# Where the end of each feature group's conditioning and the next group's first weight splits stand in the order of a decoder-layer kernel

## The chip, the cores and the metric

One program on one core of a Trainium2 chip. The metric is device time in microseconds (us) per execution. The kernel before was timed three times: 1342.04 us median, 1340.69 lowest, 1342.91 highest.

## The reference, cut to what matters

One decoder layer is computed for 288 tokens together: 256 of a prompt and 8 sequences of 4 tokens. What matters here is its head:

```
mod = silu(c) @ w_ada + b_ada                  # 2048 -> 6 * 2048, one row per request (9 rows)
sh1, sc1, g1, sh2, sc2, g2 = split(mod, 6)
h = rmsnorm(x, norm1) * (1 + sc1) + sh1        # 288 x 2048
proj = h @ w_in                                # columns: pool | z | x,B,C | dt
```

After it come a pooling mixer, a causal convolution with a state-space scan, an output projection, a gated residual, a second modulated norm and a gated feed-forward part. Everything is float32; the results are the 288 x 2048 output and the new states.

## The kernel before, in words

**Layout.** Features lie on the 128 partitions and tokens on the free axis, so x is 16 tiles (k = 0 to 15) of 128 x 288. All weights come from one flat array, `wflat`, in the order in which they are used, in loads of 128 x 1024 float32 (`load`, L232, 512 KB each, issued by SP into 14 rotating buffers, `raw`).

**Three products for one.** A weight chunk is split into two rounded parts: the high part is a cast on ACT (`split`, L241), the low part is the difference on DVE (L242; on GpSimd for the chunks in `PSPLIT`). There are three buffers for split chunks (`wsp`) in this stage. The activations are split alike into `h1k` (high by ACT L448, low by DVE L449). `mm3` then runs three matmuls on TensorE (PE) for each tile and k: high x high (L263), high x low (L264), low x high (L265).

**Feature groups.** The projection cannot start on a feature tile before that tile's scale and shift are known, and those need a 2048-long product with `w_ada`. So the 16 feature tiles are cut into six groups (`KGROUPS`): tiles 0; 1; 2-3; 4-7; 8-11; 12-15. While PE multiplies group g's features with the weights of 28 output tiles (`xbc_units`, tiles m = 0 to 27), it also computes the conditioning of group g+1 (`ada_group_units`): `VISIT` names after which tiles a *visit* is made. A visit is a run of matmuls `adag` (L343) over several `w_ada` loads.

**The end of a conditioning** is what follows the last visit: the sums go from PSUM to SBUF on ACT (`asb_g`, L298), are transposed on PE (`adat_g`, L304, or a small product, L357), and become the multiplier and the shift on DVE (`amul` L370, `ada` L373). Then `modulate1` makes the operand of the next group: on ACT `h` of the prompt tokens (L446) and the high part (L448), on DVE two operations for the short sequences (L442, L443) and the low part (L449). The program text does both once tile 28 - `MOD[g]` has been written, so MOD is how many tiles ahead of the group's end the operand is written.

**Evictions.** A finished output tile is added from PSUM to its place in SBUF by DVE (L655), two operations for most tiles (256 prompt columns, 32 others), one for a `zy` tile (for group 0 these are copies, most of them on ACT). Output tiles use two PSUM pools: 3 buffers (`mm`) for m % 7 <= 2 and 4 buffers (`aux`) for the others; the transposes of the conditioning take one of the four.

**What sets the order.** A scheduler turns the program into one list of instructions for each engine; each engine takes its list in that order. Program order gives the priority; `tc.high_priority()` raises that of what is issued inside it, as `split` and `modulate1` do. `kpo` keeps an instruction in program order. `tc.issue_after(i)` puts what is issued inside the block behind instruction i, if it is of i's engine. The change rests on these.

Of the kernel before, what the change touches and what calls it, by code (L numbers as in the profile page):

```python
# [11 lines left out]
F32 = mybir.dt.float32  # L12
F32R = mybir.dt.float32r
AF = mybir.ActivationFunctionType
ALU = mybir.AluOpType
PSUM = bass.MemoryType.PSUM

P = 128
# [6 lines left out]
NC9 = 1 + NB  # L25
# [12 lines left out]
WU = (14, 2, 6)  # L38
# [2 lines left out]
SPLIT1, SPLIT2 = 2, 2  # L41
PHASE = (128, 32, 0, 128)
YK = 2
VISIT = {1: (4, (10,)), 2: (4, (7, 15)), 3: (4, (4, 9, 14, 19)), 4: (8, (8, 19)), 5: (8, (8, 19))}
PSPLIT = {1: (1, 2, 3), 2: (0,)}
MOD = (10, 8, 6, 6, 6)
AY = 2

RA1, RA2, RB1, RB2, RB3 = 0.5, 0.4, 1.0, 1.0, 1.0
# [89 lines left out]
def kernel(ctx: ExitStack, tc, ins, outs):  # L139
    nc = tc.nc  # L140
# [8 lines left out]
    def aux(name):  # L149
        return px.tile([P, 512], F32, tag="aux", name=name)  # L150
# [31 lines left out]
    def warm_pe(n, rhs=None):  # L182

        for _ in range(n):
            nc.tensor.matmul(wps[:, :P], ones, ones if rhs is None else rhs, start=True, stop=True)

    xhi = [None]
    xlo = [None]
# [59 lines left out]
    def split_hi():  # L248
        pair = wp[0].tile([P, WSC], F32R, tag="wsp", name="wsp_xbc0_0")
        hi, lo = pair[:, WH:WH + RAWC], pair[:, WL:WL + RAWC]  # L250
        raw = load(("xbc", 0, 0))
        kpo(nc.scalar.copy(hi, raw))
        return hi, lo, raw

    def split_xbc(gi, ci, pin=False):
        (ks, ms), key = _xbc_chunks(gi)[ci], ("xbc", gi, ci)
        return ready.pop(key, None) or split(load(key), 0, len(ms) * len(ks) * P, f"xbc{gi}_{ci}",
                                             nc.gpsimd if ci in PSPLIT.get(gi, ()) else None, pin)
# [37 lines left out]
    def ada_sb(ps, nb, name, r=P, pin=lambda i: i):  # L296
        asb = kp.tile([P, 512], F32, tag="asb", name="asb_" + name)
        pin(nc.scalar.copy(asb[0:r, :nb], ps[0:r, :nb]))  # L298
        return asb

    def ada_tr(asb, nb, name, r=P):
        pt = aux("adat_" + name)
        for i in range(nb // P):
            nc.tensor.transpose(pt[:, i * r:(i + 1) * r], asb[0:r, i * P:(i + 1) * P], ident[0:r, 0:r])  # L304
        return pt
# [7 lines left out]
    def ada_group_units(gi):  # L313

        k0, gk = KGROUPS[gi]
        nj = min(2 * gk, 4)
        nb = 2 * gk * P // nj
        per = RAWC // (nj * nb)
        ps = pa.tile([P, 512], F32, tag="ada", name=f"adag{gi}")
        nq = KT // per  # L320

        def steps(q, raw):
            if gk == 1:
                for kk in range(0, per, 2):
                    for j in range(4):
                        yield j, q * per + kk + j // 2, raw[:, kk * 256 + j * P:kk * 256 + j * P + P]
            else:
                for kk in range(per):
                    for j in range(nj):
                        c = (kk * nj + j) * nb  # L330
                        yield j, q * per + kk, raw[:, c:c + nb]

        n = 0
        visit = VISIT[gi][0] if gi else 1
        for v in range(0, nq, visit):
            raws = [(q, load(("ada", gi, q))) for q in range(v, v + visit)]
            if not gi:
                yield
            begun = False
            for q, raw in raws[::-1]:  # L340
                for j, k, w in steps(q, raw):
                    with tc.high_priority() if begun else nullcontext():
                        i = nc.tensor.matmul(ps[32 * j:32 * j + 32, :nb], sc_c[:, k, :], w, start=n < 4,  # L343
                                             stop=n >= (KT if gk > 1 else KT // 2) * 4 - 4,
                                             tile_position=(0, 32 * j))
                    if begun:
                        tc.keep_in_program_order(i)
                    begun = gi > 0
                    n += 1
            if gi:  # L350
                yield
        r = 32 * nj
        pin = kpo if gi == 0 else (lambda i: i)
        if gk == 1:
            asb = ada_sb(ps, nb, f"g{gi}", pin=pin)
            pt = aux(f"adat_g{gi}")
            nc.tensor.matmul(pt[:, :r], asb[:, :nb], early[:, K_S2:K_S2 + r], start=True, stop=True)  # L357
            if gi == 0:
                warm_pe(WU[2], asb[:, 0:P])
                first.append(split_hi())  # L360
        else:
            pt = ada_tr(ada_sb(ps, nb, f"g{gi}", r), nb, f"g{gi}", r)
        for i in range(nb // P):

            o = ada[:, 0:2, k0:k0 + gk, :].rearrange("p a (b i) c -> p a b i c", b=nj // 2)[:, :, :, i, :]
            b = bada[:, 0:2, k0:k0 + gk].rearrange("p a (b i) -> p a b i", b=nj // 2)[:, :, :, i]
            src = pt[:, i * r:(i + 1) * r].rearrange("p (a b c) -> p a b c", a=2, b=nj // 2)[:, :, :, 0:NC9]
            for j in range(nj // 2):
                k = k0 + j * (nb // P) + i
                pin(nc.vector.tensor_scalar(amul[:, 0, k, :], src[:, 1, j, :], early[:, V_N1 + k:V_N1 + k + 1],  # L370
                                            nb1[:, k:k + 1], ALU.mult, ALU.add))
            o, src, b = o[:, 0], src[:, 0], b[:, 0]
            pin(nc.vector.tensor_tensor(o, src, b.unsqueeze(2).to_broadcast([P, nj // 2, NC9]), ALU.add))  # L373

    def ada_part_units(part, ay=1):
        ps = pa.tile([P, 512], F32, tag="ada", name=f"adap{part}")
# [48 lines left out]
    def normalize(k0, gk, r):  # L425
        xv = xav(k0, gk)
        kpo(nc.vector.tensor_tensor(xv, xv, r.unsqueeze(1).to_broadcast([P, gk, N]), ALU.mult))

    def modulate1(k0, gk, name):

        h = kp.tile([P, 4, N], F32, tag="hmod", name="h_" + name, bufs=2)
        xv = xav(k0, gk)
        pin = kpo if k0 == 0 else (lambda i: i)
        with tc.high_priority():
            hs = h[:, :gk, NP:N].rearrange("p k (b l) -> p k b l", b=NB)
            xs = xv[:, :, NP:N].rearrange("p k (b l) -> p k b l", b=NB)
            sa = amul[:, 0, k0:k0 + gk, 1:NC9].unsqueeze(3).to_broadcast([P, gk, NB, NL])
            sb = ada[:, 0, k0:k0 + gk, 1:NC9].unsqueeze(3).to_broadcast([P, gk, NB, NL])
            if k0 == 0:
                kpo(nc.vector.tensor_scalar(h[:, 0, 0:NP], xv[:, 0, 0:NP], amul[:, 0, 0, 0:1], ada[:, 0, 0, 0:1],  # L440
                                            ALU.mult, ALU.add))
            pin(nc.vector.tensor_tensor(hs, xs, sa, ALU.mult))  # L442
            pin(nc.vector.tensor_tensor(hs, hs, sb, ALU.add))  # L443
            for i in range(gk):
                if k0:
                    nc.scalar.activation(h[:, i, 0:NP], xv[:, i, 0:NP], AF.Identity,  # L446
                                         scale=amul[:, 0, k0 + i, 0:1], bias=ada[:, 0, k0 + i, 0:1])
                pin(nc.scalar.copy(xhi[0][k0 + i], h[:, i, :]))  # L448
                pin(nc.vector.tensor_tensor(xlo[0][k0 + i], h[:, i, :], xhi[0][k0 + i].bitcast(F32), ALU.subtract))  # L449


    class _W:
# [178 lines left out]
    def xbc_units(gi):  # L631
        k0, gk = KGROUPS[gi]
        for ci, (ks, ms) in enumerate(_xbc_chunks(gi)):
            hi, lo = split_xbc(gi, ci)
            for b, m in enumerate(ms):
                wide = gi < len(KGROUPS) - 1 and m % 7 > 2
                ps = aux(f"xbc{gi}_{m}") if wide else pm.tile([P, 512], F32, tag="mm", name=f"xbc{gi}_{m}")
                for i, k in enumerate(ks):
                    mm3(ps[:, :N], hi, lo, b * gk + i, xhi[0][k], xlo[0][k], i == 0, i == gk - 1)
                if m < XT:  # L640
                    g, r = divmod(m, 5)
                    parts = [(cvp[g][:, r, 3:3 + NP], ps[:, 0:NP]), (cvs(g)[:, r, :, 3:7], samp(ps[:, NP:N]))]
                elif m < XT + len(UEARLY):
                    u = UEARLY[m - XT]
                    parts = [(upp[:, u, 15:], ps[:, 0:NP]), (ups[:, u, :, 15:19], samp(ps[:, NP:N]))]
                else:
                    g, t = divmod(m - XT - len(UEARLY), 3)
                    parts = [(zy[g][:, t, :], ps[:, 0:N])]
                for o, v in parts:
                    if gi == 0 and m % 7 == 5:  # L650
                        nc.vector.tensor_copy(o, v)
                    elif gi == 0:
                        nc.scalar.copy(o, v)
                    else:
                        nc.vector.tensor_tensor(o, o, v, ALU.add)  # L655
                yield m
# [727 lines left out]
```

## Time and profile before

| what | value |
|---|---|
| median of three runs | 1342.04 us |
| the profiled execution's own time | 1342.67 us |
| its span in the profile | 1340.4 us |
| mean granted TensorE clock | 0.994 |
| ACT busy | 580.3 us (43%) |
| DVE busy | 818.6 us (61%) |
| GpSimd (POOL) busy | 232.0 us (17%) |
| moved by DMA | 323.25 MB, mean 241 GB/s |

PE and PEld are TensorE's matmuls and weight loads, SP the engine that issues the loads. In a table of stages, a stretch is given as from:to in us from the span's start, then its length, the busy time of each engine with its count of instructions, the granted TensorE clock (1.00 is full speed, 0.50 half), the mean busy share of the DMA engines and GB/s. In a list of instructions in order of time a row is start, length, engine, line, operation, out<-in, shapes and, in brackets, the idle time just before it and what ended it; neighbours of the same kind are merged (x2). A row of waits is engine, what waited, what it waited for, and us in total, times, longest. Names are shown without buffer numbers, so `xbc` at L263 may be a tile of one group or of the next.

Groups 0 to 5 begin on TensorE at about 19.9, 34.9, 53.0, 87.2, 141 and 192 us.

### The profile page before, as it was taken

What the parts mean: (1) busy time and instruction counts of PE and PEld (TensorE: products, weight loads), DVE (VectorE), ACT (ScalarE), POOL (GpSimd) and SP (SyncE); (2) the same over time, 40 slices, a digit from 0 to 9 for tenths busy, and PEclk for the clock granted to TensorE, in tenths of its full rate; (3) what the DMA queues carried; (4) which work ended last, traced back from release to release, by engine and by line L of the source; (5) the groups of instructions that cost most, each with busy time, mean ns of one, the idle gap of its engine ahead of it and who ended that gap; (6) DMA issues with size and microseconds to landing.
All of it is one profiled execution on the core that took longest, in us unless ns stands there. A gap on an engine that the chain in (4) does not pass through costs nothing.

```text
span 1340.4 us, 26255 instructions
## 1 busy us (share of the span) xinstructions
PE 1316.9 (98%) x10541; PEld 1230.7 (92%) x10541; DVE 818.6 (61%) x1458; ACT 580.3 (43%) x934; POOL 232.0 (17%) x420
## 2 busy tenths in 40 slices
PE   8999999999999999999999999999999999999997
PEld 7888997777778889999999999999999999999997
DVE  5675658888674448745665545666664566566553
ACT  5332434579643334533443333434433344344452
POOL 0201001223222123101221001312220011132221
PEclk9999999999999999999999999999999999999999
DMA  9997888888888967787655556656555666666641
GB/s 375 365 370 303 337 272 306 313 318 322 313 315 326 328 241 262 243 297 279 196 184 186 168 172 192 204 188 195 179 184 169 185 197 185 201 195 200 188 122 71
DMA packets 97193, 323.25 MB, mean 241 GB/s; under 512 B 10736, under 2 KB 19760, under 8 KB 97072
## 3 DMA queue, kind: packets, MB, share of 16 engines
q1 hardware_dynamic: 93168, 310.70, 67.4%
q0 software_dynamic: 3184, 9.69, 2.0%
q8 instruction: 82, 1.34, 0.4%
q10 hardware_dynamic: 720, 1.19, 0.2%
q14 instruction: 39, 0.32, 0.1%
HBM read 309.84 MB, written 10.39 MB: 239 GB/s over the span
## 4 chain that ended last, share of the span: by engine, by line
PE 94%; DVE 2%; DMA 1%; ACT 1%; issue 1%; POOL 0%; SPq 0%; DVEq 0%; POOLq 0%; ACTq 0%
PE mm_down L263 7%; PE mm_down L265 7%; PE mm_down L264 7%; PE mm_gate L263 6%; PE mm_val L263 6%; PE mm_gate L264 6%; PE mm_val L264 6%; PE mm_gate L265 6%; PE mm_val L265 6%; PE xbc L263 4%; PE xbc L264 4%; PE xbc L265 4%; PE adap L384 4%; PE mm_out L263 3%; PE mm_out L264 2%; PE mm_out L265 2%
## 5 line engine op out<-in xcount | busy, mean ns | idle before, releaser
L264 PE MATMUL mm_down<-ahl,wsp_down 128*128 128x288 f32 x688 | 201.2, 292 | 0.0
L263 PE MATMUL mm_down<-ahl,wsp_down 128*128 128x288 f32 x688 | 201.0, 292 | 0.0
L265 PE MATMUL mm_down<-ahl,wsp_down 128*128 128x288 f32 x688 | 201.0, 292 | 0.0
L263 PE MATMUL mm_gate<-h2k,wsp_gate 128*128 128x288 f32 x640 | 187.6, 293 | 0.0
L264 PE MATMUL mm_gate<-h2k,wsp_gate 128*128 128x288 f32 x640 | 187.1, 292 | 0.0
L264 PE MATMUL mm_val<-h2k,wsp_val 128*128 128x288 f32 x640 | 187.0, 292 | 0.0
L263 PE MATMUL mm_val<-h2k,wsp_val 128*128 128x288 f32 x640 | 186.9, 292 | 0.0
L265 PE MATMUL mm_gate<-h2k,wsp_gate 128*128 128x288 f32 x640 | 186.1, 291 | 0.0
L265 PE MATMUL mm_val<-h2k,wsp_val 128*128 128x288 f32 x640 | 186.0, 291 | 0.0
L242 DVE TENSOR_TENSOR wsp_down<-raw_down,wsp_down 128x1024 fp32r<-128x1024 f32 x96 | 107.3, 1117 | 119.9 <-ACT wsp_down L241 119.0
L242 DVE TENSOR_TENSOR wsp_gate<-raw_gate,wsp_gate 128x1024 fp32r<-128x1024 f32 x80 | 98.3, 1230 | 128.8 <-ACT wsp_gate L241 128.8
L241 ACT CAST wsp_down<-raw_down 128x1024 fp32r<-128x1024 f32 x96 | 92.3, 961 | 165.3 <-PE mm_down L265 114.7
L241 ACT CAST wsp_gate<-raw_gate 128x1024 fp32r<-128x1024 f32 x80 | 83.8, 1049 | 152.5 <-PE mm_gate L265 69.3
L263 PE MATMUL xbc<-h1k,wsp_xbc 128*128 128x288 f32 x448 | 133.2, 302 | 5.1 <-ACT h1k L448 3.2
L241 ACT CAST wsp_val<-raw_val 128x1024 fp32r<-128x1024 f32 x80 | 84.0, 1050 | 122.5 <-issue 107.2
L264 PE MATMUL xbc<-h1k,wsp_xbc 128*128 128x288 f32 x448 | 132.1, 297 | 0.5 <-DVE h1k L449 0.5
L263 PEld LDWEIGHTS mm_down<-ahl,wsp_down 128*128 128x128 f32 x688 | 130.1, 189 | 0.0
L265 PEld LDWEIGHTS mm_down<-ahl,wsp_down 128*128 128x128 f32 x688 | 129.2, 188 | 0.0
L264 PEld LDWEIGHTS mm_down<-ahl,wsp_down 128*128 128x128 f32 x688 | 128.8, 187 | 0.0
L265 PE MATMUL xbc<-h1k,wsp_xbc 128*128 128x288 f32 x448 | 128.5, 294 | 0.0
L263 PEld LDWEIGHTS mm_gate<-h2k,wsp_gate 128*128 128x128 f32 x640 | 120.5, 188 | 5.0 <-ACT ahl L1149 4.2
L263 PEld LDWEIGHTS mm_val<-h2k,wsp_val 128*128 128x128 f32 x640 | 120.5, 188 | 0.0
(320 smaller groups left out, 2985.0 us busy)
## 6 DMA issues: line engine op xcount, KB each, us to landing
raw_adap<-wflat SPq DMA_DIRECT2D x128, 512.0 KB, 6.1
raw_gate<-wflat SPq DMA_DIRECT2D x80, 512.0 KB, 3.5
raw_val<-wflat SPq DMA_DIRECT2D x80, 512.0 KB, 3.6
raw_ada<-wflat SPq DMA_DIRECT2D x64, 512.0 KB, 9.2
raw_xbc<-wflat SPq DMA_DIRECT2D x55, 512.0 KB, 9.1
raw_down<-wflat SPq DMA_DIRECT2D x48, 512.0 KB, 3.6
raw_out<-wflat SPq DMA_DIRECT2D x32, 512.0 KB, 6.4
raw_down<-wflat SPq DMA_DIRECT2D x32, 384.0 KB, 3.1
```

The costliest lines, as they stand in the source:

```text
L241: i = nc.scalar.copy(hi[:, :n], raw[:, a:a + n])
L242: j = (eng or nc.vector).tensor_tensor(lo[:, :n], raw[:, a:a + n], hi[:, :n].bitcast(F32), ALU.subtract)
L263: nc.tensor.matmul(ps, whi[:, w], bh, start=first, stop=False)
L264: nc.tensor.matmul(ps, whi[:, w], bl, start=False, stop=False)
L265: nc.tensor.matmul(ps, wlo[:, w], bh, start=False, stop=last)
L384: i = nc.tensor.matmul(ps[32 * j:32 * j + 32, :512], sc_c[:, k, :], raw[:, (j % 2) * 512:(j % 2) * 512 + 512], start=(k == ay - 1), stop=( ...
```

## The change

Three edits. First, the end of each conditioning (`asb_g`, `adat_g`, `amul`, `ada`) is issued at high priority. Second, in groups 1 to 5 the splits of the second and third weight chunks are put behind the last high part (on ACT) and the last low part (on DVE) of that group's operand. Third, for the conditioning of group 3, which runs in group 2, the visits stand after tiles 4, 8, 12 and 16 in place of 4, 9, 14 and 19, and the operand is written nine tiles ahead of the group's end in place of six. Nothing is added or taken away: the same instructions run in another order. The body that the first edit indents is shown by its first lines.

```diff
-VISIT = {1: (4, (10,)), 2: (4, (7, 15)), 3: (4, (4, 9, 14, 19)), 4: (8, (8, 19)), 5: (8, (8, 19))}
+VISIT = {1: (4, (10,)), 2: (4, (7, 15)), 3: (4, (4, 8, 12, 16)), 4: (8, (8, 19)), 5: (8, (8, 19))}
-MOD = (10, 8, 6, 6, 6)
+MOD = (10, 8, 9, 6, 6)
...
-        r = 32 * nj
-        pin = kpo if gi == 0 else (lambda i: i)
-        if gk == 1:
-            asb = ada_sb(ps, nb, f"g{gi}", pin=pin)
+        with tc.high_priority():
+            r = 32 * nj
+            pin = kpo if gi == 0 else (lambda i: i)
+            if gk == 1:
+                asb = ada_sb(ps, nb, f"g{gi}", pin=pin)
...
+    behind = [None, None]
...
-                pin(nc.scalar.copy(xhi[0][k0 + i], h[:, i, :]))
-                pin(nc.vector.tensor_tensor(xlo[0][k0 + i], h[:, i, :], xhi[0][k0 + i].bitcast(F32), ALU.subtract))
+                behind[0] = pin(nc.scalar.copy(xhi[0][k0 + i], h[:, i, :]))
+                behind[1] = pin(nc.vector.tensor_tensor(xlo[0][k0 + i], h[:, i, :], xhi[0][k0 + i].bitcast(F32),
+                                                        ALU.subtract))
...
-            hi, lo = split_xbc(gi, ci)
+            if gi and ci in (1, 2):
+                with tc.issue_after(behind[0].ins), tc.issue_after(behind[1].ins):
+                    hi, lo = split_xbc(gi, ci)
+            else:
+                hi, lo = split_xbc(gi, ci)
```

Three places show what this does to the order. In all of them `wsp_xbc_1` is a split of weight chunk 1 of a group, `h1k_177` and the like are operands by feature tile (177 and 178 are those of group 2, 179 to 182 those of group 3), `asb_g`, `adat_g`, `amul`, `ada` and `h_g` are the steps of the conditioning and the operand, and `cvp`, `upp`, `ups` and `zy` are where evictions go.

DVE at the end of group 1, before:

```order
L655 TENSOR_TENSOR ups<-ups,xbc_20_717 128x8x4
L370 TENSOR_SCALAR amul<-adat_g_725,early,nb_82 128x9 x2
L242 TENSOR_TENSOR wsp_xbc_1_823<-raw_xbc_1_821,wsp_xbc_1_823 128x1024
L442 TENSOR_TENSOR h_g_730<-xa_92,amul 128x2x32
L373 TENSOR_TENSOR ada<-adat_g_725,early 128x18
L655 TENSOR_TENSOR upp<-upp,xbc_21_739 128x256
L443 TENSOR_TENSOR h_g_730<-h_g_730,ada 128x2x32
L655 TENSOR_TENSOR ups<-ups,xbc_21_739 128x8x4
L655 TENSOR_TENSOR zy_195<-zy_195,xbc_22_745 128x288
L655 TENSOR_TENSOR zy_195<-zy_195,xbc_23_750 128x288
L449 TENSOR_TENSOR h1k_177<-h_g_730,h1k_177 128x288
L449 TENSOR_TENSOR h1k_178<-h_g_730,h1k_178 128x288
```

The same place in the change:

```order
L663 TENSOR_TENSOR cvp_167<-cvp_167,xbc_18_705 128x256
L371 TENSOR_SCALAR amul<-adat_g_725,early,nb_82 128x9 x2
L374 TENSOR_TENSOR ada<-adat_g_725,early 128x18
L445 TENSOR_TENSOR h_g_730<-xa_92,amul 128x2x32
L663 TENSOR_TENSOR cvp_167<-cvp_167,xbc_18_705 128x8x4
L446 TENSOR_TENSOR h_g_730<-h_g_730,ada 128x2x32
L663 TENSOR_TENSOR cvp_167<-cvp_167,xbc_19_711 128x256
```

The end of the conditioning now stands behind the first half of tile 18's eviction, not behind tile 20's, and the split of chunk 1 no longer stands between `amul` and `ada`. Further down, both low parts of `h1k` come between the two halves of tile 21's eviction, and the split of chunk 1 comes after tile 22's.

ACT at the end of group 2, before:

```order
L298 COPY asb_g_1113<-adag_835 128x256
L241 CAST wsp_xbc_6_1149<-raw_xbc_6_1147 128x1024
L241 CAST wsp_xbc_0_1187<-raw_xbc_0_1185 128x1024
L446 ACTIVATE h_g_1124<-xa_94,ada,amul 128x256 x2
L241 CAST wsp_xbc_1_1222<-raw_xbc_1_1220 128x1024
L446 ACTIVATE h_g_1124<-xa_94,ada,amul 128x256 x2
L241 CAST wsp_xbc_2_1257<-raw_xbc_2_1255 128x1024
L448 CAST h1k_179<-h_g_1124 128x288
```

And in the change:

```order
L298 COPY asb_g_1082<-adag_835 128x256
L241 CAST wsp_xbc_6_1149<-raw_xbc_6_1147 128x1024
L449 ACTIVATE h_g_1093<-xa_94,ada,amul 128x256 x2
L241 CAST wsp_xbc_0_1187<-raw_xbc_0_1185 128x1024
L451 CAST h1k_179<-h_g_1093 128x288
L449 ACTIVATE h_g_1093<-xa_94,ada,amul 128x256 x2
L451 CAST h1k_180<-h_g_1093 128x288
L451 CAST h1k_181<-h_g_1093 128x288
L451 CAST h1k_182<-h_g_1093 128x288
L241 CAST wsp_xbc_1_1222<-raw_xbc_1_1220 128x1024
```

The casts of chunks 1 and 2 of group 3 went from ahead of the operand's four high parts to behind them.

DVE at the same place, before, from the first `ada` of the conditioning on:

```order
L373 TENSOR_TENSOR ada<-adat_g_1115,early 128x2x9
L370 TENSOR_SCALAR amul<-adat_g_1115,early,nb_82 128x9
L242 TENSOR_TENSOR wsp_xbc_0_1187<-raw_xbc_0_1185,wsp_xbc_0_1187 128x1024
L370 TENSOR_SCALAR amul<-adat_g_1115,early,nb_82 128x9
L373 TENSOR_TENSOR ada<-adat_g_1115,early 128x2x9
L442 TENSOR_TENSOR h_g_1124<-xa_94,amul 128x4x32
L655 TENSOR_TENSOR zy_195<-zy_195,xbc_23_1139 128x288
L443 TENSOR_TENSOR h_g_1124<-h_g_1124,ada 128x4x32
L242 TENSOR_TENSOR wsp_xbc_1_1222<-raw_xbc_1_1220,wsp_xbc_1_1222 128x1024
L655 TENSOR_TENSOR zy_195<-zy_195,xbc_24_1152 128x288
L242 TENSOR_TENSOR wsp_xbc_2_1257<-raw_xbc_2_1255,wsp_xbc_2_1257 128x1024
L449 TENSOR_TENSOR h1k_179<-h_g_1124,h1k_179 128x288
```

And in the change, from the second pair of `amul` on:

```order
L371 TENSOR_SCALAR amul<-adat_g_1084,early,nb_82 128x9 x2
L374 TENSOR_TENSOR ada<-adat_g_1084,early 128x2x9
L445 TENSOR_TENSOR h_g_1093<-xa_94,amul 128x4x32
L663 TENSOR_TENSOR upp<-upp,xbc_20_1113 128x256
L446 TENSOR_TENSOR h_g_1093<-h_g_1093,ada 128x4x32
L663 TENSOR_TENSOR ups<-ups,xbc_20_1113 128x8x4
L663 TENSOR_TENSOR upp<-upp,xbc_21_1122 128x256
L663 TENSOR_TENSOR ups<-ups,xbc_21_1122 128x8x4
L242 TENSOR_TENSOR wsp_xbc_0_1187<-raw_xbc_0_1185,wsp_xbc_0_1187 128x1024
L452 TENSOR_TENSOR h1k_179<-h_g_1093,h1k_179 128x288
```

The conditioning is no longer cut by the split of chunk 0, and the first low part stands ahead of the splits of chunks 1 and 2. On TensorE the third and the fourth visit of group 2 keep their places, behind tiles 15 and 19, and the second moved from the end of tile 9 to the middle of tile 10. The order of SP's loads is the same up to the sixth group; GpSimd's list is the same throughout.

More of the change, by code (lines that the diff above doesn't have):

```diff
@@ L351, in ada_group_units @@
                 yield
-        r = 32 * nj
-        pin = kpo if gi == 0 else (lambda i: i)
-        if gk == 1:
-            asb = ada_sb(ps, nb, f"g{gi}", pin=pin)
[L356 to L373, printed above, removed]
+        with tc.high_priority():
[3 more added lines that the diff above has]
+                asb = ada_sb(ps, nb, f"g{gi}", pin=pin)
+                pt = aux(f"adat_g{gi}")
+                nc.tensor.matmul(pt[:, :r], asb[:, :nb], early[:, K_S2:K_S2 + r], start=True, stop=True)
+                if gi == 0:
+                    warm_pe(WU[2], asb[:, 0:P])
+                    first.append(split_hi())
+            else:
+                pt = ada_tr(ada_sb(ps, nb, f"g{gi}", r), nb, f"g{gi}", r)
+            for i in range(nb // P):
+                o = ada[:, 0:2, k0:k0 + gk, :].rearrange("p a (b i) c -> p a b i c", b=nj // 2)[:, :, :, i, :]
+                b = bada[:, 0:2, k0:k0 + gk].rearrange("p a (b i) -> p a b i", b=nj // 2)[:, :, :, i]
+                src = pt[:, i * r:(i + 1) * r].rearrange("p (a b c) -> p a b c", a=2, b=nj // 2)[:, :, :, 0:NC9]
+                for j in range(nj // 2):
+                    k = k0 + j * (nb // P) + i
+                    pin(nc.vector.tensor_scalar(amul[:, 0, k, :], src[:, 1, j, :], early[:, V_N1 + k:V_N1 + k + 1],
+                                                nb1[:, k:k + 1], ALU.mult, ALU.add))
+                o, src, b = o[:, 0], src[:, 0], b[:, 0]
+                pin(nc.vector.tensor_tensor(o, src, b.unsqueeze(2).to_broadcast([P, nj // 2, NC9]), ALU.add))
@@ L633, in xbc_units @@
         for ci, (ks, ms) in enumerate(_xbc_chunks(gi)):
-            hi, lo = split_xbc(gi, ci)
+            if gi and ci in (1, 2):
+                with tc.issue_after(behind[0].ins), tc.issue_after(behind[1].ins):
+                    hi, lo = split_xbc(gi, ci)
+            else:
+                hi, lo = split_xbc(gi, ci)
             for b, m in enumerate(ms):
```

## The prediction

> **What bounds the kernel now.** I read the page first, for the engine that carries the end; then the waits of TensorE (PE) in the stage of the feature groups, which the change touches; then a table of stretches for the granted clock; then the three busy engines in order of time at the ends of groups 1 and 2.
>
> ```profile
> PE 1316.9 (98%) x10541; PEld 1230.7 (92%) x10541; DVE 818.6 (61%) x1458; ACT 580.3 (43%) x934; POOL 232.0 (17%) x420
> ```
>
> ```profile
> PE 94%; DVE 2%; DMA 1%; ACT 1%; issue 1%; POOL 0%; SPq 0%; DVEq 0%; POOLq 0%; ACTq 0%
> ```
>
> PE is busy 98% of the span and makes 94% of the chain that ended last. The change adds and removes no matmul, so it can only win what PE loses by waiting and by a slow clock, in the part that it reorders. The longest of its waits from 18 to 180 us, in total:
>
> ```profile
> PE xbc L263 <- ACT h1k L448: 3.2, 4, 1.7
> ```
>
> Three of the four are at the start of groups 1, 2 and 3 (0.45, 0.73 and 1.68 us, below; the fourth, 0.30, is at group 0). There is none at groups 4 and 5. Stretches of 3.41 us around the two longest, and three others:
>
> ```profile
> 50.48:53.89 3.41, 1.50 (x9) 1.24 (x10) 3.21 (x11) 2.34 (x5) 0.00 (x0) 1.00 1.03 414
> 53.89:57.30 3.41, 3.41 (x17) 3.41 (x16) 2.42 (x9) 0.36 (x1) 0.00 (x0) 0.50 1.03 412
> 84.61:88.02 3.41, 1.69 (x10) 1.23 (x10) 3.30 (x7) 3.41 (x8) 0.00 (x0) 1.00 1.02 407
> 88.02:91.44 3.42, 2.95 (x12) 2.95 (x13) 2.61 (x8) 0.12 (x1) 0.00 (x0) 0.50 1.04 411
> 216.58:220.00 3.42, 2.61 (x22) 2.39 (x20) 2.41 (x6) 2.14 (x3) 1.39 (x4) 1.00 1.03 422
> 374.74:378.16 3.42, 0.93 (x6) 0.77 (x7) 3.42 (x12) 3.19 (x8) 1.71 (x2) 1.00 0.92 361
> 378.16:381.57 3.41, 3.41 (x18) 1.36 (x20) 3.20 (x12) 0.43 (x1) 0.00 (x0) 0.50 0.99 385
> ```
>
> The reader is to see that a stretch in which PE was busy for 1.50, 1.69 or 0.93 us is followed by one at a clock of 0.50, and that one with 2.61 us busy is followed by no such stretch. So the waits ahead of groups 2 and 3 cost twice: once as idle time, once as a half-speed stretch of 3.4 us.
>
> **The change part by part.** All times are on the clock of the profile before; a matmul of 288 columns starts 0.13 us after the one ahead of it.
>
> *End of group 1.* PE, ACT and DVE, in this order, one fence each:
>
> ```profile
> 49.64 0.29 PE L264 MATMUL xbc<-h1k,wsp_xbc 128*128 128x288 f32 x1
> 49.77 0.29 PE L265 MATMUL xbc<-h1k,wsp_xbc 128*128 128x288 f32 x1
> 51.66 0.37 PE L263 MATMUL xbc<-h1k,wsp_xbc 128*128 128x288 f32 x1 [1.60 <-DVE ada L373]
> ...
> 53.02 0.66 PE L263 MATMUL xbc<-h1k,wsp_xbc 128*128 128x288 f32 x3 [0.73 <-ACT h1k L448]
> ```
>
> ```profile
> 51.55 1.10 ACT L446 ACTIVATE h_g<-xa,ada,amul 128x256 f32<-128x256 f32 x2 [1.52 <-DVE ada L373]
> 52.55 0.75 ACT L448 CAST h1k<-h_g 128x288 fp32r<-128x288 f32 x2
> ```
>
> ```profile
> 46.84 1.81 DVE L655 TENSOR_TENSOR cvp<-cvp,xbc 128x256 f32<-128x256 f32 x8 [2.47 <-PE xbc L265]
> ...
> 49.00 0.47 DVE L370 TENSOR_SCALAR amul<-adat_g,early,nb 128x9 f32<-128x9 f32 x2
> 50.06 1.22 DVE L242 TENSOR_TENSOR wsp_xbc<-raw_xbc,wsp_xbc 128x1024 fp32r<-128x1024 f32 x1 [0.59 <-ACT wsp_xbc L241]
> ...
> 51.34 0.17 DVE L373 TENSOR_TENSOR ada<-adat_g,early 128x18 f32<-128x18 f32 x1
> ...
> 53.00 0.83 DVE L449 TENSOR_TENSOR h1k<-h_g,h1k 128x288 fp32r<-128x288 f32 x2 [0.20 <-ACT h1k L448]
> ```
>
> DVE did `amul` at 49.00, then waited 0.59 for ACT's cast of chunk 1, ran the split (1.22), and only then `ada` at 51.34. `ada` frees a PSUM buffer that tile 27 waits for (the 1.60), and releases `h` on ACT (1.10), whose cast releases group 2. In the change `amul` stands behind half of tile 18's eviction: about 48.25 by my estimate, since tiles 19 and 20 (0.45 each, by the 1.81 for four tiles in two halves each) no longer stand ahead. `amul` x2 and `ada` end at about 48.85, `h` and the first cast then at 50.3, 2.7 earlier than before. What is late next? The moved steps (about 0.65) now stand ahead of the evictions of tiles 18 to 20, whose buffers PE needs for tiles 24 to 26: I count 0.5 of short waits. Then the first tile of group 2 needs tile 21's buffer, whose second half is evicted behind the two low parts (0.83): DVE gets there at about 51.3. So group 2 begins at 51.35 in place of 53.02, 1.67 won. Tile 2 then waits some 0.4 for tile 23's buffer, whose eviction stands behind the split of chunk 1: 1.3 net. The waits that remain sum to 1.4, spread over 4.5 us, under 1.0 in any 3.41; that leaves PE busy for over 2.4, nearest to the row with 2.61, which no half-speed stretch follows. So the half-speed stretch goes: 3.41 at half speed is 1.7. Together 3.0; if no wait were left, 4.3; if the clock still dropped, 1.3.
>
> *End of group 2.* PE, ACT, DVE:
>
> ```profile
> 76.70 1.93 PE L343 MATMUL adag<-raw_ada,sc_c 128*32 128x256 f32 x32
> 78.56 0.40 PE L263 MATMUL xbc<-h1k,wsp_xbc 128*128 128x288 f32 x1
> ...
> 87.19 0.79 PE L263 MATMUL xbc<-h1k,wsp_xbc 128*128 128x288 f32 x4 [1.68 <-ACT h1k L448]
> 88.49 0.61 PE L264 MATMUL xbc<-h1k,wsp_xbc 128*128 128x288 f32 x1 [0.51 <-DVE h1k L449]
> ```
>
> ```profile
> 78.97 2.00 ACT L241 CAST wsp_xbc<-raw_xbc 128x1024 fp32r<-128x1024 f32 x2
> ```
>
> ```profile
> 79.88 0.48 DVE L370 TENSOR_SCALAR amul<-adat_g,early,nb 128x9 f32<-128x9 f32 x2 [1.41 <-PE adat_g L304]
> ...
> 84.24 0.17 DVE L373 TENSOR_TENSOR ada<-adat_g,early 128x18 f32<-128x18 f32 x1
> ...
> 86.84 1.23 DVE L242 TENSOR_TENSOR wsp_xbc<-raw_xbc,wsp_xbc 128x1024 fp32r<-128x1024 f32 x1
> 87.98 1.56 DVE L449 TENSOR_TENSOR h1k<-h_g,h1k 128x288 fp32r<-128x288 f32 x4
> ```
>
> The last visit ends at 78.56. Eight tiles of six matmuls (6.25), two transposes and a short wait for `asb` bring PE to the end of the group at about 85.4. Before, `ada` was finished at 84.41, behind a split, and two more splits, the last at 86.84 (1.23), stood ahead of the low part at 87.98. In the change DVE does, from 79.88 on, `amul`, one split of this group, `ada`, two `amul`, `ada` by 82.0; ACT does `h` twice (1.10), the cast of chunk 0 (1.0) and the first high part (0.37, by the 0.75 for two above) by about 83.85; DVE's split of chunk 0 ends at 84.7 and the first low part at 85.05, the other three by 86.6, while PE wants them at 85.5, 86.4 and later. No wait is left: 1.8 of start, the 0.51, and the half-speed stretch, of which PE was busy 2.95: 1.5. Sum 3.8. What gives cover here is thin: the splits of chunk 1 now end at about 88.05 on DVE, and PE wants them at 88.8.
>
> The third edit itself is priced at nothing: the visits of group 2 keep their places on PE but for one, whose loads have long landed; its effect is the earlier place of the operand, counted above.
>
> *End of group 0.* Ahead of group 1 PE waited 0.45 on the high part of its operand:
>
> ```profile
> 34.93 0.79 PE L263 MATMUL xbc<-h1k,wsp_xbc 128*128 128x288 f32 x4 [0.45 <-ACT h1k L448]
> ```
>
> ACT also evicts most tiles of group 0, so the operand's two ACT steps only change places with evictions. I take 0.6, the 0.45 and a restart; the bounds are 0 and 0.9.
>
> *Groups 4 and 5.* The same steps move, but no wait stands there. ACT now holds chunk 12's cast behind `asb`, so behind the last visit; four tiles of twelve matmuls (6.2) cover its 1.0 and DVE's 1.2. Taken as nothing.
>
> *Sum.* 0.6 + 3.0 + 3.8 = 7.4. The profiled execution took 1342.67, so one like it takes 1335.3; it lay 0.63 above the median of three, so for the median I say 1334.6. After group 3 the lists are nearly the same and TensorE is the bound, so I expect the 7.4 to be kept to the end.
>
> **The rivals.** *The waits that remain at group 2 still halve the clock.* The rows give no point between 1.69 and 2.61 us busy. For it: five short waits stay. Price 1.7: 1336.3.
>
> *The half-speed stretches have another cause and stay.* Then 1.7 and 1.5 are not won: 1337.8. Against it: all three such stretches in the rows follow a stretch half idle. [...]
>
> *Loads become the bound.* DMA engines are busy throughout up to 60 us (1.02 to 1.03 above), and PE would reach the last visit of group 2 some 4 us earlier.
>
> ```profile
> 60.79 2.48 SPq L232 DMA_DIRECT2D raw_ada<-wflat  x4
> ```
>
> ```profile
> raw_ada<-wflat SPq DMA_DIRECT2D x64, 512.0 KB, 9.2
> ```
>
> The last four loads for it were issued by 63.3 and take 9.2 in the median, so about 72.4; PE came for them at 76.7 and would come at about 72.5. Their issue waits for buffers of the first visit, which comes earlier too. For the rival they would have to stay where they were and land late by one or two loads, at 512 KB per 1.29 us (407 GB/s): 1337.2.
>
> *Given back later.* Between 200 and 400 us PE waits for DVE:
>
> ```profile
> PE pool L880 <- DVE pout L875: 2.7, 1, 2.7
> ```
>
> If DVE's chain there hung on loads and not on PE's earlier tiles, PE would wait 7.4 longer: 1342.0. Against it: the loads there are issued as PE frees buffers.
>
> *Slower: the held splits.* In groups 2 to 5 chunk 1's cast (1.0) and split (1.22) now wait for the operand. If all 2.22 came out from under cover in each, 8.9, and each wait halved the clock for 1.7, 15.7 would be lost against 7.4 won: 1350.3. It decides from the point where chunk 1's low half ends after PE asks for it; my margin is 0.7 in group 3 and 2.0 in group 2, and in groups 4 and 5 that cast waits for a buffer of the group before in any case.
>
> **How the numbers follow.** Chances: the forecast 0.60 (1333 to 1336); the clock still drops once 0.17; another cause of the half clock 0.04; loads 0.06; given back 0.07; slower 0.04; a gain beyond the forecast 0.02. The range: below, all of the bounds (0.9 + 4.3 + 4.0) and, since the later stretch at 378 could move against the stretches and not be slowed, 1.7 more: 10.9, so 1331.0. Above, the loss of the clock and a margin of 1.5 missed in group 3: 4.2 won, 1337.8, and 0.8 for the spread of the three runs: 1338.6. About 0.2% (2.7 us) is what a measurement of this kernel can tell from no change; all but the last cases beat that, with half of the loads' case: faster 0.87, same 0.09, slower 0.04.
>
> **What would show it.** Right: in the profile after, PE's waits on L448 (L451 there) at groups 2 and 3 are gone; the clock stays at 1.00 from 50 to 95 us; group 2 begins near 50.8 and group 3 near 81.5, on PE; short waits on DVE evictions (L663) appear at the end of group 1. Wrong: a half-speed stretch near 55 or 85; PE waiting for a split (L241 or L242) at the second chunk of group 2 or 3, or for a load at a visit; or group 5 beginning 7 us earlier while the feed-forward part does not.

## The result and the profile after

The change takes 1334.57 us in the median of its runs, against 1340.69 for the kernel before, run beside it: a ratio of 0.9949, with a 95% interval of 0.9937 to 0.9961. The ratio is estimated from the fast executions (one of the change's five, 4584.98 us, was slow) and is not the quotient of the two medians. The profiled execution took 1335.42 (span 1333.6) against 1342.67 (span 1340.4). The forecast was 1334.6. The page's first and fourth part:

```profile
PE 1313.3 (98%) x10541; PEld 1228.1 (92%) x10541; DVE 818.5 (61%) x1458; ACT 579.9 (43%) x934; POOL 229.1 (17%) x420
PE 95%; DVE 2%; ACT 1%; DMA 1%; POOL 0%; issue 0%; DVEq 0%; POOLq 0%; ACTq 0%
```

The instructions and their counts are the same. PE is busy 3.6 us less in all, though it does the same matmuls: fewer of them ran at half speed (one half-speed stretch between 20 us and the last 10, where the kernel before had three). All of PE's waits from 18 to 180 us, which were 3.2 on L448, 1.6 on `ada` and 0.5 on L449 among others before:

```profile
PE xbc L263 <- ACT wsp_xbc L241: 0.6, 1, 0.6
PE xbc L263 <- ACT h1k L451: 0.3, 1, 0.3
PE xbc L263 <- ACT cvp L661: 0.2, 1, 0.2
```

Stretches of 3.41 us of the change at the end of group 1, after the end of group 2, and at the wait for `pout`:

```profile
48.71:52.12 3.41, 2.82 (x20) 2.42 (x19) 3.41 (x9) 2.07 (x3) 0.00 (x0) 1.00 1.02 408
82.84:86.25 3.41, 3.41 (x29) 3.41 (x28) 3.21 (x4) 1.46 (x2) 0.00 (x0) 1.00 1.03 404
365.98:369.39 3.41, 1.19 (x10) 0.19 (x1) 3.41 (x9) 3.41 (x11) 2.60 (x3) 1.00 0.62 198
369.39:372.81 3.42, 2.96 (x13) 2.29 (x17) 2.53 (x14) 1.58 (x5) 0.00 (x0) 0.50 0.99 368
```

The clock stays at 1.00 past both ends of groups; the half-speed stretch at the wait for `pout`, which the change does not touch, is still there.

The one wait that is left at group 2, and DVE just before it:

```profile
49.94 0.37 PE L263 MATMUL xbc<-h1k,wsp_xbc 128*128 128x288 f32 x1 [0.59 <-ACT wsp_xbc L241]
```

```profile
48.55 0.41 DVE L663 TENSOR_TENSOR upp<-upp,xbc 128x256 f32<-128x256 f32 x1
48.88 0.82 DVE L452 TENSOR_TENSOR h1k<-h_g,h1k 128x288 fp32r<-128x288 f32 x2
49.62 0.18 DVE L663 TENSOR_TENSOR ups<-ups,xbc 128x32 f32<-128x32 f32 x1
```

The cast named in the bracket is that of chunk 1, which the first matmul of group 2 doesn't read. The wait ends 0.14 after the second half of tile 21's eviction (49.62 + 0.18), behind the two low parts, as the prediction had it: tile 0 takes that buffer.

**Where the time came from.** The start of group 0 differs from trace to trace (19.20 to 20.60). In before, whose group 0 starts at 19.89, the clock record first shows full speed at 6.10 us, in the change, with 19.20, at 4.17; until then the 128-column matmuls of `warm` start 0.21 apart, from then on 0.11. The table therefore gives the first matmul of each later group and the first `dttr` less the start of group 0, in us, for the traces of the kernels below:

| trace | group 1 | group 2 | group 3 | group 4 | `dttr` |
|---|---|---|---|---|---|
| before | 15.04 | 33.13 | 67.30 | 120.75 | 200.02 |
| before again (E11) | 15.04 | 33.11 | 65.72 | 118.03 | 196.92 |
| the change | 14.07 | 30.75 | 61.73 | 113.06 | 193.21 |
| the change again (E8) | 14.08 | 30.72 | 61.70 | 112.89 | 192.83 |
| E1, no priority | 15.03 | 31.15 | 61.98 | 113.32 | 192.17 |
| E2, no hold | 14.07 | 32.26 | 63.96 | 116.87 | 196.81 |
| E3, old visits | 14.05 | 30.70 | 61.68 | 112.89 | 192.76 |
| E5, hold only | 15.02 | 31.16 | 62.55 | 114.58 | 194.96 |
| E6, fill in before | 15.06 | 33.14 | 65.74 | 118.05 | 197.80 |

Between the two traces shown first (before and the change), 0.97 is won at group 1, 2.38 at group 2, 5.57 at group 3, 7.69 at group 4, and 6.81 is left at `dttr`. Up to group 3 repeats of a kernel agree to some 0.03, but for one thing: before and E11 are the same program and differ by 1.58 at group 3 and 2.72 at group 4.

### The profile page after: what moved, and what is told of

Its sections match the earlier page's. It is cut to its first block, busy times and chain, and to the rows that moved or that the text cites. A ratio compares the mean times of both kernels' runs of the same rounds, so it can differ in the third digit from the quotient of the medians.

```text
span 1333.6 us, 26265 instructions
## 1 busy us (share of the span) xinstructions
PE 1313.3 (98%) x10541; PEld 1228.1 (92%) x10541; DVE 818.5 (61%) x1458; ACT 579.9 (43%) x934; POOL 229.1 (17%) x420
## 3 DMA queue, kind: packets, MB, share of 16 engines
q10 hardware_dynamic: 720, 1.19, 0.2%
## 4 chain that ended last, share of the span: by engine, by line
PE 95%; DVE 2%; ACT 1%; DMA 1%; POOL 0%; issue 0%; DVEq 0%; POOLq 0%; ACTq 0%
PE mm_down L263 7%; PE mm_down L265 7%; PE mm_down L264 7%; PE mm_gate L263 6%; PE mm_val L263 6%; PE mm_gate L264 6%; PE mm_val L264 6%; PE mm_gate L265 6%; PE mm_val L265 6%; PE xbc L263 4%; PE xbc L264 4%; PE xbc L265 4%; PE adap L385 4%; PE mm_out L263 3%; PE mm_out L265 3%; PE mm_out L264 3%
## 5 line engine op out<-in xcount | busy, mean ns | idle before, releaser
L263 PE MATMUL xbc<-h1k,wsp_xbc 128*128 128x288 f32 x448 | 132.6, 299 | 1.2 <-ACT wsp_xbc L241 0.6
L264 PE MATMUL xbc<-h1k,wsp_xbc 128*128 128x288 f32 x448 | 130.4, 294 | 0.0
L265 PE MATMUL xbc<-h1k,wsp_xbc 128*128 128x288 f32 x448 | 126.9, 291 | 0.0
```

Of the source, the lines that this page charges most:

```text
L263: nc.tensor.matmul(ps, whi[:, w], bh, start=first, stop=False)
L264: nc.tensor.matmul(ps, whi[:, w], bl, start=False, stop=False)
L265: nc.tensor.matmul(ps, wlo[:, w], bh, start=False, stop=last)
```

## The experiments

In each, the theory is the prediction's: every end of a group has its own wait, and a stretch half idle costs a half-speed stretch behind it. Medians beside them: the kernel before took 1341.8, 1341.28 and 1341.66 in the three sets of runs, the change 1334.57 and, in E8, 1334.39.

**E1: without the high priority.**

```diff
-        with tc.high_priority():
+        with nullcontext():
             r = 32 * nj
```

> The changed kernel without its first edit (the end of each conditioning is not at high priority). My theory, each transition has its own cause: group 1 again begins behind the evictions, so the 1.0 won there is lost; at the end of group 1 the conditioning stands behind tile 20 again, 0.9 later, but no split cuts it, so PE waits some 0.3 to 0.8 more there; the end of group 2 has the same order as in the change, so its 3.9 stays and no half-speed stretch comes near 85. Total 1.3 to 1.8 slower than the change, 1336 (before 1342, change 1334.6). Rival, the priority carries the gain: the waits of 1.60 and 1.68 return with their half-speed stretches, 1341 to 1342.

Measured: 1335.49, ratio to before 0.9957 (0.9943 to 0.9970). The 0.97 at group 1 is lost, and at group 2 only 0.4 of it is left to see (31.15 against 30.75), 0.3 to 0.4 at group 4 (113.32 against 113.06 and 112.89). So the 0.97 won at the end of group 0 is mostly swallowed at the end of group 1, where the steps of the conditioning now stand ahead of evictions; E1's own wait there is

```profile
PE xbc L263 <- DVE zy L663: 0.6, 1, 0.6
```

as long as the change's. E1 is 0.9 slower than the change in the medians, less than the 1.3 to 1.8 that I expected. The rival falls: the waits of 1.60 and 1.68 stay away.

**E2: without the hold.**

```diff
-            if gi and ci in (1, 2):
+            if False:
```

> The changed kernel without its second edit (the splits of the second and third chunk are not held behind the operand). My theory: at the end of group 1 one split (1.2) again stands ahead of the low parts and of the evictions of tiles 20 and 21, at the end of group 2 two splits stand ahead of the low parts 2 to 4. PE waits 0.8 to 1.3 at each, and where the stretch falls so that PE is busy under about 2 of 3.4 us, 1.5 to 1.7 more for a half-speed stretch: 2 to 5 slower than the change, 1336.5 to 1339.5. Group 1 begins as early as in the change. Rival, the hold is only bookkeeping since the conditioning already ends early: within 0.5 of the change.

Measured: 1339.41, ratio 0.9988 (0.9974 to 1.0002). Waits and stretches of E2:

```profile
PE xbc L263 <- DVE ups L663: 1.7, 1, 1.7
PE xbc L263 <- DVE zy L663: 0.7, 1, 0.7
PE xbc L264 <- DVE h1k L452: 0.4, 1, 0.4
```

```profile
47.58:50.99 3.41, 1.93 (x11) 1.30 (x10) 3.41 (x11) 2.70 (x5) 0.53 (x1) 1.00 1.02 406
50.99:54.41 3.42, 3.13 (x13) 3.13 (x14) 3.37 (x12) 1.05 (x1) 0.00 (x0) 0.50 1.03 411
```

One split of 1.22 ahead of the low parts makes 1.7 of wait and a half-speed stretch at group 2; two splits ahead of the low parts 2 to 4 make 0.7 and 0.4 at group 3. Without this edit most of the gain is gone.

**E3: the old visits.** `VISIT[3]` and `MOD[2]` as in the kernel before.

> The changed kernel without its third edit (visits after tiles 4, 9, 14, 19 and the operand six tiles ahead again). My theory: with the first two edits the lists of DVE and ACT at the end of group 2 come out the same as in the change, so this is no slower than the change by more than its noise: 1334.6, and no wait at group 3. Rival, the third edit is what brings group 3's operand early: the wait of 1.68 ahead of group 3 returns in part, 1 to 3.8 slower, 1335.6 to 1338.4.

Measured: 1335.63, ratio 0.9950 (0.9937 to 0.9962), and every column of the table within 0.05 of E8's but `dttr` (0.07). With the other two edits the third does nothing. The prediction had priced the moved visits at nothing, and E3 bears that out; but it had counted the operand's earlier place into the 3.8 of group 2's end, and that place turns out not to be needed there either.

**E5: the hold alone.** The kernel before with the second edit and nothing else.

> The kernel before with the second edit alone (splits of the second and third chunk held behind the operand). E1 showed that without the high priority the group 2 start is as early as in the change, E2 that without the hold most of the gain goes. My theory now, the hold carries the gain: at group 2 the same wait of 0.6 as in E1 and no half-speed stretch near 54; at group 3 the conditioning is still cut by the split of chunk 0, so some 0.5 to 1.5 of wait and at most one half-speed stretch (1.5) stay. 1335.5 to 1338. Rival, the hold works only together with an early conditioning: the 1.6 ahead of tile 27 and the 1.7 ahead of group 3 stay, 1340 to 1342.

Measured: 1336.80, ratio 0.9965 (0.9953 to 0.9976). Group 2 begins where it does in E1; at group 3 one wait of 0.40 is left, and no half-speed stretch follows (granted clock of that execution 0.997, of before's 0.994). The hold alone brings 6.2 of the 7.69 at group 4 (120.75 - 114.58); against E11's trace it is 3.5 of 5.1. What it leaves, 1.5, either of the other edits gives: E1 (hold and visits) and E3 (hold and priority) are both within 0.5 of the change there.

**E4 and E6: PE's waits filled, not removed.** In the kernel before, matmuls on constants into a PSUM bank of their own; the result does not use them.

```diff
+FILL = {(1, 27): 6, (2, 0): 2, (3, 0): 7}
...
+                nf = FILL.get((gi, m), 0)
+                if nf:
+                    fp = pa.tile([P, 512], F32, tag="ada", name="fill")
+                    for _ in range(nf):
+                        with tc.issue_after(end[0].ins):
+                            end[0] = nc.tensor.matmul(fp[:, :P], ones, ones, start=True, stop=True)
```

E4 had 12, 5 and 14:

> The kernel before, with 12 matmuls of 128 columns on constants ahead of tile 27 of group 1, 5 ahead of group 2 and 14 ahead of group 3, into a PSUM bank of their own; the result does not use them. They fill PE's waits (1.60, 0.73, 1.68) and remove none of them. My theory, a stretch in which PE is idle for half of 3.4 us is followed by one at half speed: both half-speed stretches near 54 and 88 go, 1.7 + 1.5 = 3.2 won against before, 1338.8, with group 2 and 3 still beginning late. Rival, the half speed has another cause: the stretches at 0.50 stay, time as before, 1342.

It took 1342.28, ratio 1.0009 (0.9998 to 1.0021), and both half-speed stretches were gone (granted clock of the profiled execution 0.996, of before's 0.994), but the fill was twice too long: 12 such matmuls show as 24 records,

```profile
49.74 2.84 PE L647 MATMUL fill<-ones 128*128 128x128 f32 x24
```

so group 2 began at 34.13 and group 3 at 68.67 on the table's clock, 1.0 and 1.4 later than in before, and the trace tells little of the time. E6 halved it:

> The fill of E4 with half as many matmuls (6, 2 and 7), since E4's trace shows 24 PE records for 12 fills and 2.84 us in a wait of 1.60. If the half speed follows a half-idle stretch: none near 54 and 88, groups 2 and 3 begin within 0.1 of before, 3.2 is won by 95 us, and group 3's matmuls stand 3 ahead of before. What is then left at the end: if the load of chunk 6 of group 5 sets the start of dttr near 219 (E4 waited 1.8 there in place of 0.8), 1 to 2.6 of it is lost again there; 1339 to 1341. Rival, the half speed has another cause: 1342 and stretches at 0.50 near 54 and 88.

It took 1340.65, ratio 0.9992 (0.9981 to 1.0003). Its stretches behind the two ends:

```profile
50.84:54.26 3.42, 2.90 (x22) 2.49 (x21) 3.23 (x11) 2.29 (x5) 0.00 (x0) 1.00 1.02 412
54.26:57.67 3.41, 3.41 (x31) 3.25 (x29) 3.41 (x12) 1.05 (x2) 0.00 (x0) 1.00 1.04 414
84.98:88.39 3.41, 2.80 (x21) 2.37 (x20) 3.29 (x8) 2.01 (x5) 0.00 (x0) 1.00 1.01 401
88.39:91.80 3.41, 3.41 (x29) 3.41 (x28) 2.53 (x10) 1.05 (x1) 0.00 (x0) 1.00 1.03 408
```

Group 2 begins as late as before (33.14), the clock stays up, and group 4 begins 2.7 earlier than in the first trace of before (118.05 against 120.75). Taken alone this trace looks like proof that the fill did it. E11 shows that one trace isn't.

**E11: the kernel before once more**, nothing altered.

> The kernel before, nothing altered, for a second trace of it. The waits 1.60, 0.73 and 1.68 belong to its order and come again within 0.1. Whether a half-speed stretch follows each depends, by the theory, on how the 3.41 us stretches fall on them: at least one of the two comes again; at the wait for pout near 377 either way. The wait for dttr near 220 is 0.8 if it belongs to the order of before, up to 1.9 if it is the loads' luck.

Measured: 1341.88 in the median, ratio to before 1.0004 (0.9991 to 1.0017); its profiled execution took 1338.74. Its waits and its stretches:

```profile
PE xbc L263 <- ACT h1k L448: 3.1, 4, 1.7
PE xbc L263 <- DVE ada L373: 1.6, 1, 1.6
PE xbc L264 <- DVE h1k L449: 0.5, 1, 0.5
```

```profile
50.75:54.16 3.41, 1.93 (x12) 1.66 (x13) 3.22 (x12) 2.70 (x5) 0.00 (x0) 1.00 1.03 411
54.16:57.58 3.42, 3.42 (x36) 3.09 (x38) 3.42 (x11) 0.72 (x1) 0.00 (x0) 1.00 1.02 407
81.47:84.89 3.42, 2.33 (x17) 1.99 (x15) 3.42 (x8) 3.42 (x6) 0.00 (x0) 1.00 1.02 408
84.89:88.30 3.41, 2.33 (x15) 2.10 (x16) 3.29 (x8) 1.53 (x5) 0.00 (x0) 1.00 1.03 407
```

The waits are the same to 0.03, and no half-speed stretch follows. The boundaries of the stretches lie elsewhere in this execution: the wait ahead of group 3 is shared between two of them, with 2.33 busy in each, where the first trace had one with 1.69. My expectation that at least one would come again fell. So the same waits were followed by half-speed stretches in one execution and by none in the other; what differs in the rows is where the 3.41 us stretches fall on them (1.50 and 1.69 busy there; 1.93, 2.33 and 2.33 here). That this is what decides is my reading of the two. The table tells the price in these two traces of one program: group 2 lasted 34.17 with such a stretch and 32.61 without (1.56), group 3 lasted 53.45 and 52.31 (1.14).

What one trace can't tell, the granted clock of every timed execution can, since one stretch of 3.41 us at half speed lowers its mean by 0.0013 (3.41 x 0.5 / 1340). E6's twelve executions have a mean of 0.9962, the 22 of the kernel before beside them 0.9945: by this estimate some 1.3 half-speed stretches fewer in each. So filling PE's waits went with fewer such stretches. The time follows by 1.0 only (means of 1340.72 and 1341.68), which the interval doesn't tell from none; in E6's trace the first `dttr` comes 0.9 later than in E11's (197.80 and 196.92).

**E8: the change once more**, nothing altered.

> The changed kernel once more, with nothing altered, for the spread from trace to trace. Expected: 1334.6; the group starts within 0.1 of the first trace but for a common shift of up to 2 us from when the full clock comes near 5 us; the wait for dttr near 212 between 0.6 and 2.0, which would show that it is luck of the loads, not of the order; the mean distance of the output projection's matmuls 129 or 131 ns. If the dttr wait is again 1.9 to 2.0 and the spacing again 131, they belong to the kernel's order.

Measured: 1334.39, ratio 0.9954 (0.9938 to 0.9970); its profiled execution 1332.85. The group starts come again to 0.04 up to group 3. The wait for `dttr` is 1.7 again, and in before and E11 0.8 and 0.7, so it isn't the luck of one execution. It isn't settled which edit makes it: it is 0.6 in E1 (no priority), 1.6 in E3 and 2.1 in E5 (hold only). That the load behind it lands earlier or later there is my guess and was not shown. Two things differ, neither of them the program's. The wait of 2.7 for `pout` is again there, but falls on two stretches, with PE busy for 1.58 and 2.56:

```profile
365.59:369.00 3.41, 1.58 (x13) 0.32 (x5) 3.41 (x9) 3.41 (x10) 2.25 (x3) 1.00 0.49 141
369.00:372.41 3.41, 2.56 (x21) 1.62 (x25) 3.41 (x17) 1.97 (x6) 0.35 (x1) 1.00 1.00 396
```

and no half-speed stretch follows. And the output projection runs faster; its first matmuls behind two runs of `adap`, in the change and then in E8:

```profile
395.53 0.40 PE L263 MATMUL mm_out<-mixk,wsp_out 128*128 128x288 f32 x1
...
410.18 0.40 PE L263 MATMUL mm_out<-mixk,wsp_out 128*128 128x288 f32 x1
```

```profile
393.99 0.40 PE L263 MATMUL mm_out<-mixk,wsp_out 128*128 128x288 f32 x1
...
408.42 0.40 PE L263 MATMUL mm_out<-mixk,wsp_out 128*128 128x288 f32 x1
```

They stand 14.65 apart in the one and 14.43 in the other, 1.5% for the same instructions.

**E9: `dtt` ahead of the split.** Where 0.9 was given back: PE, DVE and ACT at the first `dttr` of the change.

```profile
212.41 0.32 PE L586 MATMUL dttr<-early,dtt 24*128 24x24 f32 x3 [1.95 <-DVE dtt L574]
```

```profile
210.77 1.23 DVE L242 TENSOR_TENSOR wsp_xbc<-raw_xbc,wsp_xbc 128x1024 fp32r<-128x1024 f32 x1 [1.85 <-ACT wsp_xbc L241]
211.91 0.44 DVE L574 SCALAR_TENSOR_TENSOR dtt<-dttmp 24x288 f32<-24x288 f32 x1
```

```profile
209.69 1.05 ACT L241 CAST wsp_xbc<-raw_xbc 128x1024 fp32r<-128x1024 f32 x1 [6.27 <-DMA raw_xbc<-wflat]
```

DVE holds `dtt`, which waits for nothing more, behind a split that waits 1.85 for its cast, and the cast for its load. PE's last matmul ahead of it began 8.64 earlier than in before (210.17 against 218.81), the cast 7.5 (209.69 against 217.19); the difference is what the wait grew by, from 0.81 to 1.95. E9 holds that split behind `dtt`:

```diff
...
+            elif gi == 5 and ci == 6:
+                with tc.issue_after(dtr["dtx"].ins):
+                    hi, lo = split_xbc(gi, ci)
```

> The changed kernel with the split of chunk 6 of group 5 held behind the last step of dt on DVE (L574), which stands behind that split in the change. There the split waits 1.85 for its load, and dttr on PE waits 1.95. My theory, that queue place is where 1 us of the change's gain is lost: PE's wait for dttr near 212 goes or falls below 0.5, 1.2 to 1.9 won by 216 against the change, 1333. Rival, the load itself is needed by PE: the wait moves to the first matmul of chunk 6 near 214, and the time stays at 1334.5.

Measured: 1333.62, ratio 0.9941 (0.9929 to 0.9953). PE's waits from 200 to 400:

```profile
PE pool L891 <- DVE pout L886: 2.9, 2, 2.7
PE dttr L586 <- DVE dtt L574: 0.8, 1, 0.8
PE cse L803 <- DVE ada L399: 0.7, 1, 0.7
PE cumt L596 <- DVE tok L590: 0.2, 1, 0.2
```

`dttr` begins 2.35 earlier against group 0 (190.86) than in the change. Of this only 0.45 was left at 336 us (there E9 stands 0.95 behind the change, having begun group 0 1.40 behind it), and against E8 nothing: it stands 0.96 behind, having begun 0.95 behind. The expectation held in part: the wait fell from 1.95 to 0.77, not below 0.5, and did not move to the first matmul of chunk 6. So the queue place is shown as the cause of some 1.2 of the wait; that removing it makes the kernel faster is not shown, the intervals overlap.

**E7: the wait for `pout` filled** in the change, by doing the first matmul of the output projection 18 times more (each overwrites the one before).

> The changed kernel with the first matmul of the output projection done 18 times more (2.35 us, overwritten by the last), so that PE works through the wait of 2.7 for pout near 370. By the half-idle rule the half-speed stretch near 370 goes: 1.5 to 1.7 won, 1333. Rival, the time there hangs on DVE's chain and not on PE, or the stretch is due to something else: 1334.6.

Measured: 1334.02, ratio 0.9944 (0.9930 to 0.9958). PE's wait falls from 2.7 to 0.5 and no half-speed stretch follows (granted clock of that execution 0.997, of the change's 0.996); but E8 had none either, and the median is 0.4 to 0.5 under the change's, within the noise.

**E10: E9 and E7 together.**

> E9 and the repeated matmul of E7 together: no half-speed stretch near 210 or 370 wherever the 3.41 us stretches fall. If both hold, 1332 to 1333, below the change's 1334.5 by about 2; if each only takes luck out, within 1 of the change.

Measured: 1332.41, ratio 0.9935 (0.9924 to 0.9946), the lowest median of all, with no half-speed stretch up to the last 8 us (granted clock of the profiled execution 0.997). It beats the kernel before; against the change its interval overlaps, so 2 us there is likely and not shown.

## Why the prediction was right, and where not

**The sum.** 7.4 was forecast up to the end of group 2, and 7.69 came at group 4: 0.97 at the end of group 0 (forecast 0.6, bounds 0 to 0.9), 2.97 at the end of group 1 (forecast 3.0: the start 1.41, from 2.38 less 0.97, and the half-speed stretch 1.56), and the remaining 3.75 at the end of group 2 (forecast 3.8). The first is above its bound, since I counted the wait of 0.45 and one restart, and a shorter wait on an eviction at 32.91 (0.16) went as well. Sorted by kind, the errors were larger and cancelled: with E11's trace the 7.69 is 4.97 of order (118.03 - 113.06, forecast 7.4 - 3.2 = 4.2) and 2.72 of half-speed stretches (forecast 3.2).

**Group 1's end.** Group 2 waits for tile 21's buffer behind the low parts, as foreseen. Tile 2's wait for tile 23's buffer, forecast at 0.4, did not come. Of the 0.5 of short waits at tiles 24 to 26, 0.35 came: tile 24 starts 0.25 late and tile 26 0.09, measured by the 0.13 from matmul to matmul, though only 0.09 of that shows as idle time. The waits summed to less than I feared, and the stretch was 2.82 busy.

**Group 2's end.** No wait, as foreseen. The low parts of DVE:

```profile
80.20 0.45 DVE L452 TENSOR_TENSOR h1k<-h_g,h1k 128x288 fp32r<-128x288 f32 x1
80.57 0.45 DVE L663 TENSOR_TENSOR zy<-zy,xbc 128x288 f32<-128x288 f32 x1
80.94 1.19 DVE L452 TENSOR_TENSOR h1k<-h_g,h1k 128x288 fp32r<-128x288 f32 x3
82.04 0.45 DVE L663 TENSOR_TENSOR zy<-zy,xbc 128x288 f32<-128x288 f32 x1
82.41 2.36 DVE L242 TENSOR_TENSOR wsp_xbc<-raw_xbc,wsp_xbc 128x1024 fp32r<-128x1024 f32 x2
```

Group 3 began at 80.93 and the splits of chunks 1 and 2 followed the low parts under its cover, so the slower rival did not come.

**The other parts.** Groups 4 and 5 were taken as nothing, and group 4 lasted 55.43 in both traces. Loads did not become the bound: no visit waits in the list of waits above.

**The step that failed: "I expect the 7.4 to be kept to the end."** 0.9 of it was lost at the first `dttr`. That was the rival "given back later" in a small form: I had priced it at all or nothing, at the wait for `pout` (2.7 before and after, so nothing), and passed over a wait of 0.8 for `dtt` that stood behind a load. What else differs is not the change's: between two matmuls of the output projection (at 382.58 and 469.35 in before, 374.94 and 462.47 in the change) another 0.76 went, at its slower spacing in that execution (130.9 ns on average from matmul to matmul, 129.7 in before), and 0.69 was won ahead of group 0 (19.89 to 19.20). So it is luck that the median met the forecast to 0.03. The forecast also took the first three runs' 1342.04 for the kernel before, which took 1340.69 beside the change: the win in the medians of those runs is 6.1, not 7.4.

**The step that was right for this trace only: the half-speed stretches.** I took 3.2 for their going, as if the kernel before always had them. E11 is the same kernel without them. What the order itself wins is the difference of the two traces that have none: 118.03 - 112.89 = 5.1 at group 4 and 4.1 at `dttr`. The rest of the 7.1 between the medians (about 1341.6 and 1334.5) should come, by my estimate, from executions in which the stretches of 3.41 us fall badly on before's waits. The granted clock of each execution fits that, here for the clocks that both kernels had, with the number of executions and their mean time in us:

| granted clock | kernel before | the change |
|---|---|---|
| 0.994 | 25, 1342.17 | 1, 1338.45 |
| 0.995 | 15, 1340.87 | 2, 1336.88 |
| 0.996 | 17, 1340.21 | 4, 1334.69 |
| 0.997 | 5, 1339.00 | 1, 1333.39 |
| all, mean clock | 73, 1341.46, 0.9947 | 11, 1334.75, 0.9963 |

At the same clock the change is 3.7 to 5.6 ahead, which is the order's part. The means are 6.7 apart, and the clock differs by 0.0016 in the mean, 1.2 half-speed stretches fewer in each execution of the change; at 1.1 to 1.6 apiece they are worth 1.3 to 1.9. Eleven executions make this an estimate. The rival "the clock still drops once" did not come in any of the traces of the change.

**The half-idle rule.** What follows is measured on single stretches, between the first 20 us and the end of the program. Those with PE busy for 0.93 (before), 1.04 (E6) and 1.19 us (the change), all at the wait for `pout`, were followed by one at 0.50; those at full speed with 2.33 (E11, twice), 2.56 (E8), 2.61 (before) and 2.82 (the change) by one at 1.00. In the last 12 us of the change, left out here, one with 2.42 was followed by 0.50. From 1.49 to 1.93 it went either way: 1.50 and 1.69 in before, 1.63 in E4 and 1.69 and 1.93 in E2 were followed by 0.50, but 1.58 in E8, 1.74 in E4, 1.93 in E11 and 1.49 in the change, at `dttr`, by 1.00:

```profile
208.97:212.38 3.41, 1.49 (x12) 1.26 (x10) 1.61 (x3) 2.13 (x3) 0.81 (x3) 1.00 1.00 408
```

What decides there stays open. In E2 one wait of 1.7, with PE busy for 1.93 of the 3.41 us, was followed by a half-speed stretch.

## What to carry to other kernels

Where a queue runs in order, ask of each instruction in it what it waits for: a split that nobody needs yet, queued ahead of the operand of the next stage, cost 1.22 of DVE time and with it a PE wait of 1.7 in E2, and holding it back won most of what three edits won together (6.2 of 7.69 at group 4). Raising the priority of a chain helps the chain and delays what it overtakes; the gain at one transition can be gone at the next, as 0.97 at group 1 was 0.4 at group 2 here. And before a cost that comes in one execution and not in the next, as the half-speed stretches behind groups 1 and 2 did in before and E11, is put into a sum, or a fix of it is believed, take a second trace of the same kernel, and compare the granted clock of all its timed executions.

## What the runs showed of the hardware

- In the clock records of before and the change, all that lies between the first full speed (at 6.10 and 4.17 us) and the last stretch at half speed lasts whole multiples of 3.41 us: in turn 14 at full and 1 at half speed, 9 and 1, 84 and 1, and 279 at full speed in before; 107 and 1, and 279 in the change. They lie differently on the program: the half-speed stretch at the wait of 2.7 for `pout` began 0.93 us after that wait's end in before (378.16 and 377.23) and 0.46 ahead of it in the change (369.39 and 369.85); in E8 the same wait was followed by none. Between before and E11 a half-speed stretch cost 1.56 us at group 2 and 1.14 at group 3.
- The output projection's matmuls ran 1.5% apart in two executions of one program (14.65 and 14.43 us for the same run of instructions, the change and E8), at a granted clock of 1.00 in both in the rows from 412 to 453 us. The mean distance was 131 ns in the change, 130 in before and 129 in E8. The cause was not tried.
- Group 0 began at 19.20 us in the change, 19.89 in before and 20.60 in E9, a spread that is a fifth of the gain which was to be measured.
